# Pulling the down-projection turns of a segment apart by up units, and counting GpSimd's transfers in the kernel's own scheduler

## The chip, the cores and the metric

The kernel runs on one core of a Trainium2 chip. The metric is the device time of one execution in microseconds (us), lower is better; each value below is the median of runs of the same program. The core has five engines with their own instruction queues: TensorE (PE, with its weight loads shown as PEld), VectorE (DVE), ScalarE (ACT), GpSimd (POOL) and SyncE (SP). In this kernel SP issues the loads of weights, and POOL issues the transfers that add into DRAM.

## The reference: what is computed

One decoder block on 256 tokens of width 2048, all in float32. A conditioning vector c gives six vectors of shift, scale and gate (`mod = silu(c) @ w_ada + b_ada`).

```
h = modulate(rms_norm(x), sh1, sc1);  proj = h @ w_in          # 2048 -> 6144: q k v, and gb gc xt
attn = causal attention of 8 heads with normalised q, k;  conv = gb * causal_dwconv(gc * xt)
x = x + g1 * (concat(rms_norm(attn), rms_norm(conv)) @ w_out)
h2 = modulate(rms_norm(x), sh2, sc2)
u = causal_dwconv(h2 @ w_ffn_up);  u_gate, u_up = split(u)     # 2048 -> 11264
x = x + g2 * ((silu(u_gate) * u_up) @ w_ffn_down)              # 5632 -> 2048
```

## The kernel before

Every product is made from two halves of each operand: a weight tile `raw` of 1 MB is loaded by SP, ACT rounds it to `hi` (L299, `split_hi`), DVE subtracts to get `lo` (L308, `split_lo`), and PE adds three products (hi times hi, hi times the rest of the other operand, lo times hi). The activations are split in the same way.

The work is a list of 208 *steps* (the code calls them `slots`), each with one weight tile and its matmuls, in the order in which PE runs them:

- 48 steps of `w_in`, in the order of `CFG['turns']`. An entry names a 512-column group (`q0`, `q1`, `k0`, ...; a bare letter means both groups at once) and a range of 128-row blocks of the input. A group whose next entry is more than three steps away (`near`) has its sum taken out of PSUM: `evac_in` copies it the first time (ACT) and adds to it afterwards (DVE, L502).
- 16 steps of `w_out`. Here the attention, the short convolution and the second normalisation run beside the matmuls.
- 12 steps that begin six *up units* (units 0 to 5, the first half of the input rows).
- From step 76 on (`F0`), the order of `CFG['plan']`. An integer is an up unit: 512 columns of `w_ffn_up`, four steps of 4 blocks (two for units 0 to 5, which have begun), into four PSUM banks `z`. Units 2n and 2n+1 hold the gate and the up part of the same columns, so the pair gives two *groups* (2n and 2n+1) of rows for the down projection. A pair `(seg, fp)` is a *down turn*: it multiplies the groups of one segment with one half (fp) of the columns of `w_ffn_down`. Segments 0, 1, 2 have 8, 6 and 4 groups; the last 4 groups go through the *tail*, eight steps at the end.

In a down turn a group is done either with a step `c` (24 matmuls), or, for the letter `S` in `CFG['forms']`, with a seven-product scheme in two steps: `r` (9 matmuls), then sums of the weight blocks on DVE in place (`sums_of`, L319 to L321), then `T` (12 matmuls). A turn fills eight banks; each is copied by ACT (`evac_q`, L907) and added by POOL into a DRAM accumulator (L909). After the last segment POOL reads the eight sums of a half back (`load_q`, L923), DVE joins them to four tiles (`join`, L931), `gate_down` multiplies them by the gate g2 (L963, L965), and POOL adds the output rows.

When an up unit's last step is through, a *chain* turns its banks into operands of the down projection: `up_sum_a` copies on ACT (L804), `up_sum_v` adds on DVE (L816), `up_conv` on ACT (L842, L840) and `up_taps` on DVE (L856), `up_gate` on DVE (L864), `up_hi` on ACT (L868), `up_lo` on DVE (L872, it writes `gl`). `up_sum_v` is what frees the four banks.

The conditioning weights `w_ada` are interleaved: an entry of `CFG['ada']` is [which of the six, first block, columns, on PE, first step, span, ...]; its tiles are loaded by SP and consumed by DVE (L375, L377) or PE. For the last gate g2 (entry 5) the two numbers are the first and the last up unit beside which it is consumed. The gate g2 is then spread over the partitions by two matmuls in front of four chosen up steps, `CFG['spread']`, pairs of [unit, its step]: a bank is taken, PE writes it (L1715, L1716), and ACT copies it out (L1724, `spread_copy`), which frees the bank.

From step 76 on, the order of the instructions on ACT, DVE and POOL is chosen at build time by a list scheduler in the kernel. Every operation is an `Op` with an engine, a cost, what it depends on, a due time, and the banks and tiles it takes and frees. At each turn of its loop it takes, on each engine, the operation that could start now with the earliest due time:

```python
            start = max([clock[o.e], o.nb] + [d.end + (0.05 if d.e != o.e else -1.0 if d.e == "PE" else 0.0) for d in o.deps] + [sorted(res[k])[n - 1] for k, n in o.need.items() if n]
                        + ([landed.get(o.key, 0.0)] if o.key is not None else []))
            late = max(0.0, start - clock[o.e] - CFG["slack"])
            rank = (late > 0, late if late > 0 else o.due)
```

When a weight tile will have landed is guessed by `arrive`: each load takes 2.7 us of one DMA clock. The engines then run what they were given in that order, whatever really lands when. There are 8 PSUM banks, 6 buffers for `raw`, and in the scheduler's account 12 small tiles.

Of the kernel before, what the change touches and what calls it, by code (L numbers as in the profile page):

```python
# [16 lines left out]
S = 256  # L17
# [11 lines left out]

CFG = {'ada': [[0, 12, 512, False, 17, 4], [4, 8, 512, False, 66, 9], [0, 4, 512, True, 4, 6],
# [4 lines left out]
 'bufs': [38, 6, 6, 3, 5],  # L37
# [5 lines left out]
 'fill': [[3, 12]],  # L43
 'fill_at': [0, 14, 11],
 'tr3': 0,
 'keep': {},
 'spin': [0, 0, 0, 0, 0, 0],
 'plan': [6, 0, 1, 7, 2, 3, 8, 4, 5, 9, (0, 0), (0, 1), 10, 11, 12, 13, 14, 15, (1, 0), (1, 1), 16, 17, 18, 19, (2, 1), (2, 0), 20, 21],
 'tail': [(0,36,4),(1,36,4),(2,36,4),(0,40,4),(1,40,4),(2,40,4),(3,36,4),(3,40,4)],
 'slack': 0.05,  # L50
 'taps': [1, 0, 0],
 'utaps': 2,
 'utlag': 1,
 'sslag': 1,
 'split': [6, 8],
 'segs': [8, 6, 4, 4],
 'forms': ['cScScScc', 'cScScc', 'cScc'],
 'back_q': [-17, -12],
 'join': [30.0, 10.0],
 'tiles': 12,  # L60
 'free0': 4,
 'spread': [[19, 2], [19, 3], [20, 2], [20, 3]],
 'heads': [2, 7, 8, 4, 5, 5, 4, 4],
 'head_steps': [1, 1, 2, 3, 5],
 'conv': [[1, 3, 3, 2, 6, 9, 8, 9], [1, 2, 3, 2, 1, 3, 5, 5]],
# [11 lines left out]
 'tr': [3, 7, 2],  # L77
 'part': 2,
 'up': [[0, 2, 3], [0, 2, 3], [0, 2, 3], [0, 2, 3]],
 'gate': [30, 30, 10, 10],  # L80
 'cls': {'add': 2,
         'h2_rest': 1,
         'att_n': 1,
# [45 lines left out]
 'direct': [4, 0],  # L129
 'spill': [8, 2],  # L130
 'back': [-10, -9, -1, -6],
 'x_first': [1, 2, 3, 4, 5, 9, 10, 12, 13, 15, 16, 19, 21, 23, 24, 28, 31, 39, 43, 45, 46, 48, 49, 50, 51, 55, 56,
             58, 59, 64, 65],
 'h_act': True,
 'h_lag': 0,
 'hi_late': [5, 8, 12, 14, 15, 16, 17, 18, 19, 20, 21, 23, 27, 28, 35, 39, 40, 45, 49, 53, 56, 58, 61, 65, 66, 67, 68, 72, 74, 76, 77, 78, 80, 81, 82, 84, 85, 86, 88, 89, 90, 92, 93, 94, 120, 122, 123, 125, 126, 127, 129, 133, 134, 136, 137, 138, 139, 143, 163, 165, 166, 167, 169, 171, 172, 174, 190, 191, 193, 195, 198, 199, 201, 202, 204],
 'first_hi': True,
 'xn_ahead': [6],
 'cut': [4, 4],
# [5 lines left out]
def tile_block(  # L145
# [138 lines left out]

    splits, halfway = [], []

    kind, held, ready_w = {}, {}, {}

    def half_tile(tag, i):
        t, n = (tag, N_HL) if i < DEEP or (i - DEEP) % 4 else ("raw", N_RAW)  # L290
        return sb.tile([P, 4, 512], F32R, tag=t, bufs=n, name=tag)

    def split_hi(nk, gate=None, i=0):
        t = held.pop(i - 1) if kind.get(i) == "T" else take(slots[i][0] if clock else None)
        if gate is not None and not clock:
# [148 lines left out]
    slots, tasks, extra = [], {}, {}  # L444
# [163 lines left out]
    def rows_of(t, f):  # L608
        return out[0, t * P:(t + 1) * P, f * 512:(f + 1) * 512]
# [294 lines left out]
    def evac_q(seg, fp, n):  # L904
        if True:
            e = t2k(f"e{fp}{n}")
            act(e, qb.pop((seg, fp, n)), AF.Copy, scale=-1.0 if n in ("a", "c00", "c10") else 1.0)  # L907
            if (fp, n) in qd:
                nc.gpsimd.dma_start(qd[fp, n], e, accum_op=ALU.add)  # L909
            else:  # L910
                qd[fp, n] = dram.tile([P, 512], F32, name=f"q{fp}{n}")
                nc.gpsimd.dma_start(qd[fp, n], e)

# [44 lines left out]
    def gate_down(f):  # L958
        assert (G2, f) in gB
        for t in range(2):  # L960
            d = dacc[t, f]
            if f % 2:
                V.tensor_tensor(out=d, in0=d, in1=gB[G2, f], op=ALU.mult)  # L963
            else:
                V.scalar_tensor_tensor(out=d, in0=d, scalar=-1.0, in1=gB[G2, f], op0=ALU.mult, op1=ALU.mult)  # L965
            if f < 2:
                nc.gpsimd.dma_start(rows_of(t, f), d, accum_op=ALU.add)
            else:
                nc.gpsimd.dma_start(d, rows_of(t, f), accum_op=ALU.add)
# [10 lines left out]
    def down_turn(seg, fp, ga, form):  # L980

        a11, a12, a22 = (1, 0), (0, 0), (0, 1)
        todo = []
        for i, e in enumerate(form):
            g = ga + i

            def tok(j, t, g=g):
                return tuple(v[:, t * P:(t + 1) * P] for v in gT[2 * g + j])

            if e == "c":  # L990
                todo.append(("c", [(f"c{t}{f}", (tok, j, t), 2 * j + f) for f in range(2) for t in range(2) for j in range(2)], g))
            else:
                todo.append(("r", [("a", (tok, *a11), 2), ("c00", (tok, *a12), 0), ("c01", (sT, g, 3), 1)], g))
                todo.append(("T", [("c10", (tok, *a22), 0), ("7", (sT, g, 1), 1), ("6", (sT, g, 2), 2), ("5", (sT, g, 0), 3)], g))
        first, last = {}, {}
        for i, (_, ps_, _) in enumerate(todo):
            for j, (n, _, _) in enumerate(ps_):
# [64 lines left out]
        a += n  # L1062
    F0 = N_OUT + NS * cut[0] // 4
    for (a, b), form in zip(SEGS, CFG["forms"]):
        assert b - a == len(form)
        seven |= {a + i for i, e in enumerate(form) if e == "S"}
        for n, g in enumerate(sorted(seven & set(range(a, b)))):
            wide_st[g] = n < 3
    for grp in range(NS):
# [567 lines left out]

    done_1 = {}
    up_ops(F0 - 1)
    for i in range(F0, len(slots)):  # L1640
        j = i + LA
        for j in ([j] if j < len(slots) else []):
            raw = slots[j][0]
            nk = slots[j][1]
            d = [pe.get(j - 4)]
            if kind.get(j) == "T":
                d.append(sum_op[j - 1])
            if j in gated:
# [27 lines left out]
        for seg, fp, n in outs_at.get(i, []):  # L1676
            if fp is None:
                f = n
                Op("DVE", 1.3 if f < 3 else 1.5, lambda f=f: evac_down(f), [pe[i], prev["gB", f]] + (g_op["gd", f] if f > 1 else []), due=tid[i + 1] + 5,
                   free={"b": 2}, need={"t": 2}, out=2 if f < 2 else 0)  # L1680
            else:
                a = Op("ACT", 0.48, lambda seg=seg, fp=fp, n=n: evac_q(seg, fp, n), [pe[i]], need={"t": 1}, free={"b": 1}, out=1)
                freeing.append((i, a, 1))
                prev["q", fp] = a
            if (seg, n) == (len(CFG["forms"]) - 1, "c11"):
                b = None
                for r in range(3):
# [124 lines left out]
```

## Time and profile before

| | |
|---|---|
| time before, median of 3 runs | 1169.33 us (1168.83 to 1169.68) |
| the profiled execution, own time | 1167.0 us |
| its span, first to last instruction | 1165.2 us |
| mean granted TensorE clock | 0.998 of full speed |
| PE busy | 1143.1 us (98%) |
| DVE / ACT / POOL busy | 960.6 / 733.9 / 68.2 us |
| DMA | 334.76 MB, mean 287 GB/s |

The profiled execution is 2.3 us shorter than the median of the runs without a profile, and its time is 1.8 us longer than its span.

### The profile page before, as it was taken

Reading aid. Unit: us, or ns where it says so; the run is one execution under the profiler, and the core shown is the slowest. Engines: PE = TensorE matmul, PEld = TensorE weight load, DVE = VectorE, ACT = ScalarE, POOL = GpSimd, SP = SyncE. Lnnn points to the kernel's source line nnn. Section 1 sums busy time; section 2 is a strip of 40 time slices with the busy share of each in tenths; the row PEclk is TensorE's granted clock in tenths of the full one; section 3 lists DMA queues with packets and bytes.
Section 4 is the critical chain, followed back from the end, with each engine's and each line's share of the span. In section 5 each row is a group of like instructions: output and inputs, shape, how many; then the busy total and the mean of one; then the engine's idle time right before and its main releaser. Section 6 shows DMA issues by size and latency. Waiting matters only on the chain.

```text
span 1165.2 us, 15759 instructions
## 1 busy us (share of the span) xinstructions
PE 1143.1 (98%) x6079; PEld 967.0 (83%) x6079; DVE 960.6 (82%) x996; ACT 733.9 (63%) x1134; POOL 68.2 (6%) x100
## 2 busy tenths in 40 slices
PE   5999999999999999999999999999999999999998
PEld 3677778888887889988888888888888888888787
DVE  4889989999999978878888987589878658775685
ACT  6645365567785565569879765477666648674551
POOL 1000000000000000000000001100001210014302
PEclk9999999999999999999999999999999999999999
DMA  9999989999899799965564576888767997569965
GB/s 363 406 415 412 408 321 367 385 346 346 288 341 339 254 329 324 384 222 181 183 201 161 179 262 236 327 327 288 266 213 218 262 302 278 198 178 315 306 249 108
DMA packets 140442, 334.76 MB, mean 287 GB/s; under 512 B 6592, under 2 KB 15252, under 8 KB 136016
## 3 DMA queue, kind: packets, MB, share of 16 engines
q1 hardware_dynamic: 129728, 311.45, 74.0%
q0 software_dynamic: 9344, 20.17, 7.6%
q10 hardware_dynamic: 1296, 2.16, 0.5%
q8 instruction: 47, 0.77, 0.2%
q14 instruction: 27, 0.22, 0.1%
HBM read 315.92 MB, written 17.83 MB: 286 GB/s over the span
## 4 chain that ended last, share of the span: by engine, by line
PE 88%; DMA 7%; DVE 2%; ACT 2%; issue 1%; SPq 0%; DVEq 0%; ACTq 0%
PE z L1044 24%; PE z L1047 12%; PE z L1030 4%; PE qc L1008 3%; PE qc L1007 3%; PE qc L1006 3%; DMA raw<-in_w_ffn_up_dram 2%; DMA raw<-in_w_ada_dram 2%; DVE lo L308 1%; DMA raw<-in_w_ffn_down_dram 1%; PE mk L490 1%; PE mk L491 1%; PE mk L488 1%; PE ada L371 1%; PE mq L490 1%; PE mq L491 1%
## 5 line engine op out<-in xcount | busy, mean ns | idle before, releaser
L308 DVE TENSOR_TENSOR lo<-raw,hi 128x2048 fp32r<-128x2048 f32 (+1 forms) x207 | 465.9, 2257 | 107.5 <-ACT hi L299 104.3
L299 ACT ACTIVATE hi<-raw 128x2048 fp32r<-128x2048 f32 (+1 forms) x207 | 390.3, 1892 | 251.6 <-DMA raw<-in_w_ffn_up_dram 60.2
L1044 PE MATMUL z<-h,hi 128*128 128x512 f32 x1280 | 301.0, 392 | 2.1 <-ACT ada L1724 2.1
L1044 PEld LDWEIGHTS z<-h,hi 128*128 128x128 f32 x1280 | 238.7, 189 | 50.6 <-ACT ada L1724 2.5
L377 DVE SCALAR_TENSOR_TENSOR ada<-raw,csil,ada 128x512 f32<-128x512 f32 (+3 forms) x167 | 195.6, 1176 | 23.4 <-DMA raw<-in_w_ada_dram 19.9
L1047 PEld LDWEIGHTS z<-h,lo 128*128 128x128 f32 x1280 | 159.2, 192 | 3.3
L1047 PE MATMUL z<-h,lo 128*128 128x256 f32 x1280 | 160.4, 283 | 0.0
L1008 PE MATMUL qc<-lo,gh 128*128 128x512 f32 x216 | 84.2, 390 | 0.2 <-DVE lo L308 0.2
L1006 PE MATMUL qc<-hi,gl 128*128 128x512 f32 x216 | 84.0, 389 | 0.0
L1007 PE MATMUL qc<-hi,gh 128*128 128x512 f32 x216 | 84.0, 389 | 0.0
L840 ACT ACTIVATE tap<-ub,fc 128x256 f32<-128x256 f32 x176 | 75.0, 505 | 0.0
L856 DVE TENSOR_TENSOR uy<-tap,uy 128x510 f32<-128x510 f32 x88 | 60.2, 687 | 8.3 <-ACT tap L840 3.8
L804 ACT ACTIVATE ub<-z 128x256 f32<-128x256 f32 x112 | 34.4, 385 | 39.4 <-PE z L1044 33.1
L842 ACT ACTIVATE uy<-ub,fc,fc 128x256 f32<-128x256 f32 x88 | 48.1, 601 | 9.9 <-DVE ub L816 7.7
L1008 PEld LDWEIGHTS qc<-lo,gh 128*128 128x128 f32 x216 | 40.6, 188 | 9.4 <-DVE lo L308 1.1
L1007 PEld LDWEIGHTS qc<-hi,gh 128*128 128x128 f32 x216 | 40.6, 188 | 8.4
L1006 PEld LDWEIGHTS qc<-hi,gl 128*128 128x128 f32 x216 | 40.5, 188 | 8.4
L1030 PE MATMUL z<-h,hi 128*128 128x256 f32 x256 | 46.6, 284 | 0.4 <-ACT h L740 0.2
L1030 PEld LDWEIGHTS z<-h,hi 128*128 128x128 f32 x256 | 40.0, 192 | 0.8 <-ACT h L740 0.5
L816 DVE TENSOR_TENSOR ub<-z,ub 128x256 f32<-128x256 f32 x96 | 33.9, 416 | 7.6 <-ACT ub L804 7.6
L1030 PE MATMUL z<-h,lo 128*128 128x256 f32 x128 | 36.2, 283 | 0.0
L355 POOL MEMSET ada<- 128x2048 f32 x2 | 3.6, 1814 | 517.4 <-DVE lo L308 438.2
(509 smaller groups left out, 1776.4 us busy)
## 6 DMA issues: line engine op xcount, KB each, us to landing
raw<-in_w_ada_dram SPq DMA_DIRECT2D x96, 1024.0 KB, 7.0
raw<-in_w_ffn_up_dram SPq DMA_DIRECT2D x88, 1024.0 KB, 5.2
raw<-in_w_in_dram SPq DMA_DIRECT2D x47, 1024.0 KB, 7.9
raw<-in_w_ffn_down_dram SPq DMA_DIRECT2D x44, 1024.0 KB, 6.3
raw<-in_w_out_dram SPq DMA_DIRECT2D x16, 1024.0 KB, 6.3
q<-e POOLq DMA_DIRECT2D x18, 256.0 KB, 7.2
q0c<-e0c POOLq DMA_DIRECT2D x12, 256.0 KB, 8.0
q1c<-e1c POOLq DMA_DIRECT2D x12, 256.0 KB, 7.5
```

The costliest lines, as they stand in the source:

```text
L299: act(hi[:, :nk], t[:, :nk], AF.Copy)
L308: V.tensor_tensor(out=lo[:, :nk], in0=t[:, :nk], in1=hi[:, :nk].bitcast(F32), op=ALU.subtract)
L377: V.scalar_tensor_tensor(out=self.acc, in0=t[:, j, :], scalar=csil[:, i:i + 1], in1=self.acc, op0=ALU.mult, op1=ALU.add)
L840: act(z[d - 1][:, s], ub[unit][w][:, s], AF.Copy, scale=fcols[2 - d][:, i:i + 1])
L842: act(y[:, s], ub[unit][w][:, s], AF.Identity, bias=fcols[3][:, i:i + 1], scale=fcols[2][:, i:i + 1])
L856: V.tensor_tensor(out=pair(y)[:, :, d:], in0=pair(z[d - 1])[:, :, :256 - d], in1=pair(y)[:, :, d:], op=ALU.add)
L1006: mm(qb[seg, fp, n], y, hi[:, b], start=first[n] == (i, j), stop=False)
L1007: mm(qb[seg, fp, n], x, hi[:, b], start=False, stop=False)
L1008: mm(qb[seg, fp, n], x, lo[:, b], start=False, stop=last[n] == (i, j))
L1030: mm(o, w[:, j, a], h2T[k + j][:, v * 256:v * 256 + 256], start=begins and j == 0 and w is hi and not v, stop=ends and j == 3 and w is lo)
L1044: mm(zp[grp][ft], hi[:, j, ft * P:(ft + 1) * P], h2T[k + j], start=begins and j == 0, stop=ends and j == 3)
L1047: mm(zp[grp][ft][:, :256], lo[:, j, ft * P:(ft + 1) * P], h2T[k + j][:, :256], start=False, stop=False)
```

## The change

The list of steps is permuted, and the scheduler is told of more. No operation of the arithmetic is added; the counts of matmuls are the same. Part by part:

- `plan`: unit 10 moves between the two turns of segment 0, units 18 and 19 move between the two turns of segment 2, the turns of segment 1 change places, and units 0 and 6 change places at the start.
- `forms`: in segment 1 the seven-product steps are groups 2 and 4 of the turn in place of 1 and 3.
- `spread`: the steps [19, 2], [19, 3], [20, 2], [20, 3] become [19, 2], [20, 1], [20, 2], [21, 2].
- `moved`: the scheduler's DMA clock is advanced by 1.4 us for each of POOL's adding transfers and by 0.65 us for each of its plain ones.
- `load_q` depends on all eight copies of the turn, not on the last one made; `join` of the second half may come 13 us after its turn in place of 10; `gate_down` of block 1 is due later (42 for 30); the scheduler's `slack` is 0.1 for 0.05.
- `turns`: the first two entries change places; `g1` and `k1` move up and `v` 2 to 4 moves down among the early ones; `x0` 8 to 16 moves up by four steps. `ada`: four entries start or end one or two steps (units) earlier or later. `x_first` and `hi_late` (the order of ACT's rounding within a step) change in a few numbers.
- New letters `r` and `T` in a form would allow the two steps of a group to be apart; the forms in use don't have them.

```diff
-CFG = {'ada': [[0, 12, 512, False, 17, 4], [4, 8, 512, False, 66, 9], [0, 4, 512, True, 4, 6],
-         [5, 0, 2048, False, 9, 17], [3, 8, 512, False, 54, 8], [1, 4, 512, False, 3, 7],
+CFG = {'ada': [[0, 12, 512, False, 18, 3], [4, 8, 512, False, 64, 9], [0, 4, 512, True, 4, 6], [4, 0, 1024, False, 23, 22],
+         [0, 8, 512, True, 11, 12], [0, 2, 256, True, 0, 5], [5, 0, 2048, False, 8, 16], [3, 8, 512, False, 54, 7],
...
- 'turns': [['g', 0, 2], ['c', 0, 2], ['v', 0, 2], ['x', 0, 2], ['q', 0, 4], ['c', 2, 4], ['k', 0, 4], ['g', 2, 4],
-           ['x', 2, 4], ['x1', 4, 8], ['x0', 4, 8], ['v', 2, 4], ['g1', 4, 8], ['k1', 4, 8], ['v0', 4, 8],
+ 'turns': [['c', 0, 2], ['g', 0, 2], ['v', 0, 2], ['x', 0, 2], ['q', 0, 4], ['c', 2, 4], ['k', 0, 4], ['g', 2, 4],
+           ['x', 2, 4], ['x1', 4, 8], ['g1', 4, 8], ['x0', 4, 8], ['k1', 4, 8], ['v', 2, 4], ['v0', 4, 8],
...
- 'plan': [6, 0, 1, 7, 2, 3, 8, 4, 5, 9, (0, 0), (0, 1), 10, 11, 12, 13, 14, 15, (1, 0), (1, 1), 16, 17, 18, 19, (2, 1), (2, 0), 20, 21],
+ 'plan': [0, 6, 1, 7, 2, 3, 8, 4, 5, 9, (0, 0), 10, (0, 1), 11, 12, 13, 14, 15, (1, 1), (1, 0), 16, 17, (2, 1), 18,
+          19, (2, 0), 20, 21],
- 'slack': 0.05,
+ 'slack': 0.1,
...
- 'forms': ['cScScScc', 'cScScc', 'cScc'],
+ 'forms': ['cScScScc', 'ccScSc', 'cScc'],
- 'join': [30.0, 10.0],
+ 'join': [30.0, 13.0],
- 'spread': [[19, 2], [19, 3], [20, 2], [20, 3]],
+ 'spread': [[19, 2], [20, 1], [20, 2], [21, 2]],
...
- 'gate': [30, 30, 10, 10],
+ 'gate': [30, 42, 10, 10],
...
+    def moved(us):
+
+        clock["DMA"] = max(clock["DMA"], clock["now"] + 1.0) + us
...
             if (fp, n) in qd:
                 nc.gpsimd.dma_start(qd[fp, n], e, accum_op=ALU.add)
+                moved(1.4)
             else:
+                moved(0.65)
...
             nc.gpsimd.dma_start(t, qd[fp, n])
+            moved(0.65)
...
                 nc.gpsimd.dma_start(d, rows_of(t, f), accum_op=ALU.add)
             else:
                 nc.gpsimd.dma_start(d, rows_of(t, f), accum_op=ALU.add)
+                moved(1.4)
...
-                prev["q", fp] = a
-            if (seg, n) == (len(CFG["forms"]) - 1, "c11"):
+                left_q.setdefault((seg, fp), []).append(a)
+            if seg == len(CFG["forms"]) - 1 and len(left_q[seg, fp]) == 8:
...
-                    a = Op("POOL", (3.0, 2.0, 3.0)[r], lambda fp=fp, r=r: load_q(fp, r), [prev["q", fp], b],
+                    a = Op("POOL", (3.0, 2.0, 3.0)[r], lambda fp=fp, r=r: load_q(fp, r), left_q[seg, fp] + [b],
```

## Rows read from the trace of the kernel before

**Rows 1.** Part 1 of the page: busy time of an engine, its share of the span, instructions.

```profile
PE 1143.1 (98%) x6079; PEld 967.0 (83%) x6079; DVE 960.6 (82%) x996; ACT 733.9 (63%) x1134; POOL 68.2 (6%) x100
```

**Rows 2.** The list of waits of PE over the whole span: who waited for whom, total us, times, longest.

```profile
PE ada L371 <- DMA raw<-in_w_ada_dram: 9.2, 3, 7.3
PE pv_ccol L212 <- DMA vcb<-in_c_dram: 4.0, 1, 4.0
PE z L1044 <- ACT ada L1724: 2.1, 1, 2.1
...
PE qc L1008 <- DVE lo L308: 0.2, 1, 0.2
```

**Rows 3.** The timeline of PE in units 20 and 21 (start, duration, what, count, and in brackets the idle time before it and what ended it). A line merges neighbours of one kind.

```profile
1077.67 0.40 PE L1715 MATMUL adab<-adah,onesr 128*128 128x512 f32 x1
...
1083.74 0.39 PE L1715 MATMUL adab<-adah,onesr 128*128 128x512 f32 x1
...
1086.11 4.50 PE L1044 MATMUL z<-h,hi 128*128 128x512 f32 x19
1092.71 4.82 PE L1044 MATMUL z<-h,hi 128*128 128x512 f32 x13 [2.10 <-ACT ada L1724]
1097.36 2.92 PE L1047 MATMUL z<-h,lo 128*128 128x256 f32 x23
```

**Rows 4.** The same view in unit 14 and 15, where PE doesn't wait.

```profile
841.38 4.00 PE L1047 MATMUL z<-h,lo 128*128 128x256 f32 x32
845.21 7.44 PE L1044 MATMUL z<-h,hi 128*128 128x512 f32 x32
852.49 4.00 PE L1047 MATMUL z<-h,lo 128*128 128x256 f32 x32
```

**Rows 5.** Busy time by stretches of 1 us around the wait: the stretch, its length, busy us (instructions) of PE, PEld, DVE, ACT, POOL, then the granted TensorE clock, the busy share of the DMA engines and GB/s.

```profile
1091.00:1092.00 1.00, 0.00 (x0) 0.00 (x0) 1.00 (x2) 1.00 (x1) 0.00 (x0) 1.00 1.06 414
...
1093.00:1094.00 1.00, 1.00 (x3) 0.81 (x3) 1.00 (x1) 1.00 (x1) 1.00 (x3) 0.50 0.66 256
1094.00:1095.00 1.00, 1.00 (x4) 0.71 (x4) 1.00 (x2) 1.00 (x3) 1.00 (x4) 0.50 0.88 154
...
1096.00:1097.00 1.00, 1.00 (x6) 0.81 (x5) 1.00 (x2) 0.00 (x0) 1.00 (x3) 0.91 0.98 133
```

**Rows 6.** The timeline of ACT over the same stretch.

```profile
1084.77 1.92 ACT L299 ACTIVATE hi<-raw 128x2048 fp32r<-128x2048 f32 x1 [4.09 <-DMA raw<-in_w_ffn_up_dram]
1086.59 0.58 ACT L1724 ACTIVATE ada<-adab 128x512 f32<-128x512 f32 x1
1090.26 1.91 ACT L299 ACTIVATE hi<-raw 128x2048 fp32r<-128x2048 f32 x1 [3.08 <-DMA raw<-in_w_ffn_up_dram]
1092.08 0.58 ACT L1724 ACTIVATE ada<-adab 128x512 f32<-128x512 f32 x1
```

**Rows 7.** The DMA view of 1040 to 1095 us: queue, packets, MB, share of the time of 16 engines (q1 is SP's, q0 is POOL's), and an issuing group with its count, KB each and median us from issue to landing.

```profile
q1 hardware_dynamic: 5103, 10.74, 53.1%
q0 software_dynamic: 2997, 6.40, 52.6%
...
raw<-in_w_ffn_up_dram SPq DMA_DIRECT2D x8, 1024.0 KB, 12.0
```

**Rows 8.** The same view of 960 to 1040 us, where POOL's queue moved nothing.

```profile
q1 hardware_dynamic: 6549, 17.22, 61.3%
...
raw<-in_w_ffn_up_dram SPq DMA_DIRECT2D x8, 1024.0 KB, 5.2
```

**Rows 9.** The chains behind unit 17 (968 to 996 us) and unit 21 (from 1115 us), from the timelines of PE, ACT and DVE. In the first row 16 matmuls are the end of unit 17 and 16 the start of unit 18; the chain does two groups, so a row with x2 or x4 holds one or both.

```profile
975.31 7.44 PE L1044 MATMUL z<-h,hi 128*128 128x512 f32 x32
...
982.28 1.16 ACT L804 ACTIVATE ub<-z 128x256 f32<-128x256 f32 x4
...
988.15 1.47 DVE L856 TENSOR_TENSOR uy<-tap,uy 128x510 f32<-128x510 f32 x2
989.66 0.69 DVE L864 TENSOR_TENSOR uy<-uy,uy 128x512 f32<-128x512 f32 x1
...
994.59 1.29 DVE L872 TENSOR_TENSOR gl<-uy,gh 128x512 fp32r<-128x512 f32 x2
...
1115.86 1.19 ACT L804 ACTIVATE ub<-z 128x256 f32<-128x256 f32 x4
...
1118.19 1.41 DVE L816 TENSOR_TENSOR ub<-z,ub 128x256 f32<-128x256 f32 x4
...
1118.72 1.10 ACT L842 ACTIVATE uy<-ub,fc,fc 128x256 f32<-128x256 f32 x2
1119.70 1.71 ACT L840 ACTIVATE tap<-ub,fc 128x256 f32<-128x256 f32 x4
...
1128.64 1.13 ACT L868 ACTIVATE gh<-uy 128x512 fp32r<-128x512 f32 x2
...
1130.57 1.29 DVE L872 TENSOR_TENSOR gl<-uy,gh 128x512 fp32r<-128x512 f32 x2
```

**Rows 10.** Of the early part: the only wait of PE from 55 to 440 us; the adds of `evac_in` into one letter's sums (min/median/max ns, first and last start); DVE's `lo` for step 66 with the idle time before it; three of the four DVE instructions that consume one 512-column tile of `w_ada`.

```profile
PE z L1030 <- ACT h L740: 0.2, 1, 0.2
...
L502 DVE TENSOR_TENSOR pa_g<-mg,pa_g x12: 680/682/685, 91.7 to 327.4; 128x512 f32<-128x512 f32 x12
...
437.52 4.58 DVE L308 TENSOR_TENSOR lo<-raw,hi 128x2048 fp32r<-128x2048 f32 x2 [2.29 <-ACT hi L299]
...
446.16 2.33 DVE L377 SCALAR_TENSOR_TENSOR ada<-raw,csil,ada 128x512 f32<-128x512 f32 x3
```

More of the change, by code (lines that the diff above doesn't have):

```diff
@@ L47 @@
  'spin': [0, 0, 0, 0, 0, 0],
- 'plan': [6, 0, 1, 7, 2, 3, 8, 4, 5, 9, (0, 0), (0, 1), 10, 11, 12, 13, 14, 15, (1, 0), (1, 1), 16, 17, 18, 19, (2, 1), (2, 0), 20, 21],
- 'tail': [(0,36,4),(1,36,4),(2,36,4),(0,40,4),(1,40,4),(2,40,4),(3,36,4),(3,40,4)],
- 'slack': 0.05,
+ 'plan': [0, 6, 1, 7, 2, 3, 8, 4, 5, 9, (0, 0), 10, (0, 1), 11, 12, 13, 14, 15, (1, 1), (1, 0), 16, 17, (2, 1), 18,
+          19, (2, 0), 20, 21],
+ 'tail': [(0, 36, 4), (1, 36, 4), (2, 36, 4), (0, 40, 4), (1, 40, 4), (2, 40, 4), (3, 36, 4), (3, 40, 4)],
+ 'slack': 0.1,
  'taps': [1, 0, 0],
@@ L131 @@
  'back': [-10, -9, -1, -6],
- 'x_first': [1, 2, 3, 4, 5, 9, 10, 12, 13, 15, 16, 19, 21, 23, 24, 28, 31, 39, 43, 45, 46, 48, 49, 50, 51, 55, 56,
-             58, 59, 64, 65],
+ 'x_first': [1, 2, 3, 4, 5, 9, 10, 12, 13, 15, 16, 20, 21, 23, 24, 28, 31, 39, 43, 45, 46, 48, 49, 50, 51, 55, 56, 58,
+             59, 64, 65],
  'h_act': True,
  'h_lag': 0,
- 'hi_late': [5, 8, 12, 14, 15, 16, 17, 18, 19, 20, 21, 23, 27, 28, 35, 39, 40, 45, 49, 53, 56, 58, 61, 65, 66, 67, 68, 72, 74, 76, 77, 78, 80, 81, 82, 84, 85, 86, 88, 89, 90, 92, 93, 94, 120, 122, 123, 125, 126, 127, 129, 133, 134, 136, 137, 138, 139, 143, 163, 165, 166, 167, 169, 171, 172, 174, 190, 191, 193, 195, 198, 199, 201, 202, 204],
+ 'hi_late': [5, 8, 12, 15, 16, 17, 19, 20, 21, 23, 27, 28, 35, 39, 40, 45, 49, 53, 55, 56, 58, 61, 65, 66, 67, 68, 72,
+             74, 76, 77, 78, 80, 81, 82, 84, 85, 86, 88, 89, 90, 92, 93, 94, 120, 122, 123, 125, 126, 127, 129, 133,
+             134, 136, 137, 138, 139, 143, 163, 165, 166, 167, 169, 171, 172, 174, 190, 191, 193, 195, 198, 199, 201,
+             202, 204],
  'first_hi': True,
@@ L285, in tile_block @@
     splits, halfway = [], []
-    kind, held, ready_w = {}, {}, {}
+    kind, held, ready_w, opener = {}, {}, {}, {}
     def half_tile(tag, i):
@@ L293, in split_hi @@
     def split_hi(nk, gate=None, i=0):
-        t = held.pop(i - 1) if kind.get(i) == "T" else take(slots[i][0] if clock else None)
+        t = held.pop(opener[i]) if kind.get(i) == "T" else take(slots[i][0] if clock else None)
         if gate is not None and not clock:
@@ L982, in down_turn @@
         a11, a12, a22 = (1, 0), (0, 0), (0, 1)
-        todo = []
-        for i, e in enumerate(form):
-            g = ga + i
+        todo, g, begun = [], ga, []
+        for e in form:
             def tok(j, t, g=g):
@@ L991, in down_turn @@
                 todo.append(("c", [(f"c{t}{f}", (tok, j, t), 2 * j + f) for f in range(2) for t in range(2) for j in range(2)], g))
-            else:
+            if e in "rS":
                 todo.append(("r", [("a", (tok, *a11), 2), ("c00", (tok, *a12), 0), ("c01", (sT, g, 3), 1)], g))
-                todo.append(("T", [("c10", (tok, *a22), 0), ("7", (sT, g, 1), 1), ("6", (sT, g, 2), 2), ("5", (sT, g, 0), 3)], g))
+                begun.append((("T", [("c10", (tok, *a22), 0), ("7", (sT, g, 1), 1), ("6", (sT, g, 2), 2),
+                                     ("5", (sT, g, 0), 3)], g), len(slots) + len(todo) - 1))
+            if e in "TS":
+                t, o = begun.pop(0)
+                opener[len(slots) + len(todo)] = o
+                todo.append(t)
+            if e != "T":
+                g += 1
+        assert not begun
         first, last = {}, {}
@@ L1064, in tile_block @@
     for (a, b), form in zip(SEGS, CFG["forms"]):
-        assert b - a == len(form)
-        seven |= {a + i for i, e in enumerate(form) if e == "S"}
+        assert b - a == len(form.replace("T", ""))
+        seven |= {a + i for i, e in enumerate(form.replace("T", "")) if e in "rS"}
         for n, g in enumerate(sorted(seven & set(range(a, b)))):
@@ L1639, in tile_block @@
     up_ops(F0 - 1)
+    left_q = {}
     for i in range(F0, len(slots)):
@@ L1646, in tile_block @@
             if kind.get(j) == "T":
-                d.append(sum_op[j - 1])
+                d.append(sum_op[opener[j]])
             if j in gated:
@@ L1680, in tile_block @@
                    free={"b": 2}, need={"t": 2}, out=2 if f < 2 else 0)
+                continue
             else:
```

7 rows, old and new, of the table CFG are left out of this document.

## The prediction

> **What bounds the kernel now.** I read the busy shares first, then the waits of PE, then the pitch of its matmuls, and last the timelines around the one long wait. PE is busy for 98% of the span [rows 1], but a busy row can hide stalls, since a matmul's record is longer than its pitch. So the pitch decides: where PE doesn't wait, 32 matmuls of 512 columns take 852.49 - 845.21 = 7.28 us from the first start to the next kind's first start, 0.2275 us each, and 32 of 256 columns take 3.83 us, 0.12 us each [rows 4]. A full step of an up unit (16 of each) is thus 5.56 us, and no order of the same matmuls makes it less. What an order can win is only the time in which PE doesn't keep this pitch.
>
> The waits say where that is [rows 2]. Of about 16 us, 13.2 lie at the start (the first vector and the first `w_ada` tiles), before anything this change moves can matter. From 55 to 440 us PE waits 0.2 us in all [rows 10]. After that there is one wait of any size: 2.1 us for ACT's `spread_copy` (L1724). Another of 0.2 us is for a `lo` in a down turn.
>
> The timeline of PE gives the whole price of that wait [rows 3]. The 32 matmuls of 512 columns that end unit 20 and begin unit 21 start at 1086.11, the next kind at 1097.36: 11.25 us for what takes 7.28 elsewhere [rows 4], so 3.97 us are lost. 2.10 of them are the wait. The rest is slow matmuls behind it: 13 in 4.65 us where 13 x 0.2275 = 2.96 would do. The granted clock was 1.00 in the idle stretch and 0.50, the 1.2 GHz level, for the stretches after 1093, back towards 1.00 in 1096 to 1097 [rows 5]: PE had been idle for 2.1 us before it fell, and at work again since 1092.71 when it rose.
>
> Why the wait: PE needs the fourth bank of unit 21, and the bank is still held by a spread sum. The two last spreads were made at 1077.67 and 1083.74 [rows 3], but ACT copied them out at 1086.59 and 1092.08, over 8 us later each [rows 6]. Ahead of each copy in ACT's order stands a rounding of `raw` that waits for its load, 4.09 and 3.08 us. The loads are late because from 1040 to 1095 POOL's queue takes 52.6% of the DMA engines' time beside SP's 53.1%, and a 1 MB load takes 12.0 us from issue to landing [rows 7]; without POOL's traffic it took 5.2 [rows 8]. That traffic is the sums of two adjacent turns of segment 2 and their reading back.
>
> **The change, part by part.**
>
> *`spread`.* The copies at [20, 2] and before now have two steps, 2 x 5.56 = 11.1 us, until unit 21 asks for its fourth bank. Even if a copy again starts 8.9 us after its spread began (1086.59 - 1077.67) and takes 0.58, it ends 1.6 us ahead. The one at [21, 2] is wanted back only in the tail, more than 11 us later, since unit 20's four banks are free by then. Worth: 3.97 us, the whole loss; if the copy were late by two steps, 0. I take 3.97. The four pairs of matmuls are the same as before, 0.
>
> *Units 18 and 19 between the turns of segment 2, and `join` at 13.* POOL's 6.40 MB of 1040 to 1095 are some 24 transfers of 256 KB, 52.6% of 55 us = 28.9 us of all engines, 1.2 us each. Eight adds and eight reads back of the first turn leave this stretch: 19 of 28.9 us. The loads of units 20 and 21 should then land in 5 to 8 us. That gives PE nothing beyond the 3.97 us, since it has no other wait there. The moved 19 us fall in units 18 and 19, four steps each, 44 us.
>
> *Segment 2 directly behind unit 17.* This is the price I fear. The turn `cScc` uses unit 17's first group in its third weight block, that is after 24 + 9 + 12 = 45 matmuls, 10.2 us after unit 17's end. Its chain, by its own durations, is 1.19 + 1.41 + 2.69 (L842 and L840, 1118.72 to 1121.41) + 1.47 + 0.69 + 0.6 + 0.68 = 8.7 us [rows 9]: no stall. As it ran before, the first `gl` was done 16.3 us after unit 17's end (978.95 to 995.27), and for unit 21 15.4 us after the chain began [rows 9]: a stall of 5.2 to 6.1 us. Neither had to hurry: group 16 was wanted 8 x 5.56 + 10.2 = 54.7 us later, and unit 21's groups after three steps of the tail, 72 x 0.2275 = 16.4 us, and were ready just then. So the scheduler fits a chain to its due time, and I take a value near the lower end: 10.7 us, a stall of 0.5. Both ends stay for the range.
>
> *Unit 10 between the turns of segment 0, segment 1's order and forms.* PE lost 0.2 us in all the down turns by the list of waits [rows 2]. At most that is won; the cover is what ACT and DVE have ready, and if it fails in one step the cost is that step's lateness. 0.
>
> *`moved`, `left_q`, `slack`, `gate`.* They change the order that the scheduler writes, not an operation. Where PE keeps its pitch this is worth 0, and at most the 3.97 us counted above; a wrong order costs what the next part but one says.
>
> *Early turns and loads.* One `evac_in` fewer adds twice 0.682 us less on DVE [rows 10]; PE waits 0.2 us in this stretch, so it is worth 0 to 0.2. The first tile of `w_ada` entry [4, 8] is now consumed ahead of step 66's `lo`: some 3.1 us (2.33 for three of four instructions) where DVE idled 2.29 [rows 10], so that `lo` ends about 0.8 us later; for PE the bounds are 0 and 3.1 us, and I take 0, since DVE's idle time takes three quarters of it and PE shows no wait on DVE here. Unit 0 wants the upper half of the normalised input two steps sooner than unit 6 did, and the entry that feeds it is moved two steps up: 0. g2's tiles end one unit sooner, which helps unit 17.
>
> Sum against the profiled execution: 1167.0 - 3.97 + 0.5 = 1163.5. The runs without a profile lie 2.3 us above it, which I carry over: 1169.33 - 3.5 = 1165.8.
>
> **The rivals.**
>
> *The chain is late* (slower). If unit 17's chain runs as slowly as both chains on record, PE stalls 5.2 to 6.1 us and, as behind the wait of 2.1 us, 1.7 us more at the lower clock: 1169.33 - 3.97 + 6.9 to 7.8 = 1172.3 to 1173.2. For it: the record. Against it: the due times. It decides from a chain of 14.8 us on (stall 4.6 + 1.7 = 6.3); between 11.5 and 14.8 the result is no change.
>
> *The jam moves.* POOL's 19 us of transfers meet the loads of units 18 and 19, those land late, and the copy for [19, 2] or the release of a unit's banks waits behind them on ACT as before. It costs what it cost there, about 4 us: 1169.3 to 1169.8. For it: the two queues took even shares of the engines whatever their sizes [rows 7]. Against it: from 960 to 1040 SP's queue used 61.3% [rows 8], so there is room for most of the 19 us in 44. The Trainium skill, "DMA: Bandwidth & Descriptors", section "Queues, rings and completion order", states that each engine takes turns between the queues that have work, a packet at a time. The even shares above agree. By that rule alone the collision isn't removed but moved, and the sum would be this rival's.
>
> *It doesn't do what it says.* Another copy stands behind a late load and the same wait stays at unit 21: 1169.3. The 1.6 us to spare speak against it.
>
> *More is won.* The new order also clears the 0.2 us waits and something at the start: 1163.5 to 1164.5.
>
> **How the numbers follow.** Forecast case (wait gone, new stalls under 1.5 us) 0.52, its own range 1164.5 to 1167.0; chain late 0.15, a third of it between the signs; jam moves 0.15; wait stays 0.08; more won 0.07; early part 1 to 2 us worse, 0.03. A measurement tells this kernel from no change at about 0.2%, 2.3 us: below 1167.0 is faster, above 1171.7 slower. Faster: 0.52 + 0.07 and a little of the jam, 0.60. Slower: two thirds of the late chain and a little, 0.13. Same: 0.27. The range leaves out the late chain and the lower half of "more won": 1164.0 to 1171.0.
>
> **What would show it.** PE's list of waits without `ada L1724`, the clock 1.00 around unit 21, loads of units 20 and 21 at 5 to 8 us, and POOL's bytes spread over both stretches. A wait of PE in the turn behind unit 17 on `gl` (L872) shows the late chain, one in units 18 and 19 on ACT the moved jam. The forecast is wrong if either is above 2 us, or if PE waits between 60 and 500 us for more than 1 us.

## The result, and the profile after

After takes 1162.38 us (1161.86 to 1162.58, 6 runs), and before beside it 1168.93 (1167.28 to 1169.68, 6 runs); over the 93 runs of before that the experiments below added, it takes 1167.4 (1165.1 to 1170.6). The ratio is 0.9945 [0.9932, 0.9958], and in a second comparison (e13, after unchanged, expected at 1161.9 to 1162.6) 0.9954 [0.9941, 0.9968]: some 5 us, 0.5% faster, and faster than the range that I gave. The profiled execution of after has a span of 1160.8 us and an own time of 1162.58, against 1165.2 and 1167.0.

The busy times on the page, and under them the list of waits of PE over the whole span, as in [rows 1, 2]:

```profile
PE 1141.7 (98%) x6079; PEld 967.2 (83%) x6079; DVE 959.3 (83%) x994; ACT 734.0 (63%) x1134; POOL 67.8 (6%) x100
```

```profile
PE ada L378 <- DMA raw<-in_w_ada_dram: 8.6, 3, 7.5
PE pv_ccol L215 <- DMA vcb<-in_c_dram: 4.3, 1, 4.3
PE mq L497 <- DVE adaz L415: 0.6, 1, 0.6
PE mc L559 <- ACT h L1516: 0.4, 1, 0.4
PE z L1048 <- ACT h L747: 0.3, 1, 0.3
```

The line for L1724 is gone, and so is the 0.2 us for `lo` in a down turn. In this profile nothing behind 430 us waits any more (the second profile of after, e13's, has one wait of 0.3 us for a `lo` at 737 us). The timelines of PE and ACT through units 20 and 21 (L1062 is before's L1044, L1744 its L1724) answer [rows 3, 6]:

```profile
1077.66 0.40 PE L1735 MATMUL adab<-adah,onesr 128*128 128x512 f32 x1
...
1085.64 7.44 PE L1062 MATMUL z<-h,hi 128*128 128x512 f32 x32
1092.92 4.00 PE L1065 MATMUL z<-h,lo 128*128 128x256 f32 x32
```

```profile
1080.64 1.92 ACT L306 ACTIVATE hi<-raw 128x2048 fp32r<-128x2048 f32 x1 [5.17 <-DMA raw<-in_w_ffn_up_dram]
1082.46 0.58 ACT L1744 ACTIVATE ada<-adab 128x512 f32<-128x512 f32 x1
```

The 32 matmuls at the unit's border take 1092.92 - 1085.64 = 7.28 us, the undisturbed pitch of [rows 4], where before took 11.25. The copy still stands behind a rounding that waits 5.17 us for its load, and comes 4.8 us after its sum, but nobody wants that bank yet. The DMA view of 1040 to 1095 us, and then of 990 to 1040, answers [rows 7, 8]:

```profile
q1 hardware_dynamic: 4884, 9.71, 50.6%
q0 software_dynamic: 1744, 3.66, 31.6%
...
raw<-in_w_ffn_up_dram SPq DMA_DIRECT2D x8, 1024.0 KB, 7.7
```

```profile
q0 software_dynamic: 1792, 4.20, 33.3%
...
raw<-in_w_ffn_up_dram SPq DMA_DIRECT2D x6, 1024.0 KB, 12.0
```

POOL's bytes are spread over both stretches, and the slow loads have moved: 7.7 us for units 20 and 21 (12.0 before), 12.0 for units 18 and 19. Last, the chain behind unit 17, which answers [rows 9]: PE's timeline, where the first row begins the turn and the second is the first matmul that needs unit 17's first group, and then DVE's.

```profile
978.94 0.39 PE L1024 MATMUL qc<-hi,gl 128*128 128x512 f32 x1
...
989.14 0.39 PE L1024 MATMUL qc<-hi,gl 128*128 128x512 f32 x1
```

```profile
987.25 0.68 DVE L879 TENSOR_TENSOR gl<-uy,gh 128x512 fp32r<-128x512 f32 x1
```

The first `gl` is done at 987.93, 9.0 us after the unit's end at 978.94. PE wants it at 989.14, so 1.2 us are to spare.

### The profile page after: what moved, and what is told of

The parts are those of the page before. It is cut to its first block, busy times and chain, and to the rows that moved or that the text cites. A ratio compares the mean times of both kernels' runs of the same rounds, so it can differ in the third digit from the quotient of the medians.

```text
span 1160.8 us, 15739 instructions
## 1 busy us (share of the span) xinstructions
PE 1141.7 (98%) x6079; PEld 967.2 (83%) x6079; DVE 959.3 (83%) x994; ACT 734.0 (63%) x1134; POOL 67.8 (6%) x100
## 4 chain that ended last, share of the span: by engine, by line
PE 94%; DMA 3%; DVE 1%; ACT 1%; issue 0%; SPq 0%; DVEq 0%; ACTq 0%
PE z L1062 25%; PE z L1065 13%; PE qc L1025 4%; PE qc L1024 4%; PE qc L1026 4%; PE z L1048 4%; DMA raw<-in_w_ada_dram 2%; PE mk L497 1%; PE mk L498 1%; PE mk L495 1%; PE ada L378 1%; PE mq L497 1%; PE mq L498 1%; PE mq L495 1%; PE mv L497 1%; PE mc L497 1%
## 5 line engine op out<-in xcount | busy, mean ns | idle before, releaser
L1062 PE MATMUL z<-h,hi 128*128 128x512 f32 x1280 | 299.5, 390 | 0.0
L1062 PEld LDWEIGHTS z<-h,hi 128*128 128x128 f32 x1280 | 237.7, 188 | 47.8
```

What stands on the lines that cost most here:

```text
L1062: mm(zp[grp][ft], hi[:, j, ft * P:(ft + 1) * P], h2T[k + j], start=begins and j == 0, stop=ends and j == 3)
```

## The experiments

All times are medians. Kernels e1 to e4, e5 to e8, e9 to e12, e13 to e16 and e17 to e18 ran together, each group on one chip, with before beside them at 1167.04, 1167.45, 1167.79, 1167.49 and 1167.39.

**Where the 2.3 us lie: e1**, before unchanged.

> The kernel before, unchanged, for the span and the clock of each of its runs and for a second profile. Theory A: the 2.3 us by which the runs of before exceed its profiled execution are longer stalls at late loads, in the program itself. Then time minus span is 1.8 us in every run, as in both profiles so far, the spans spread from 1165 to 1168, and the longer ones have a mean clock below 0.998. Theory B: they lie around the program (launch, measuring). Then the spans stay within 0.5 us of 1165.2 and time minus span is 2 to 4 us in the longer runs.

Measured: 1167.02 (1165.11 to 1169.53, 12 runs). Over the 93 runs of before the spans go from 1163.3 to 1168.7 and time minus span has a median of 1.86 us (86 of the 93 lie between 1.79 and 2.2, the longest is 3.1). The 21 runs with a span under 1164.5 have a mean clock of 0.9997, the 33 of 1166 or more 0.9972. The second profile shows where most of it goes: the list of waits of PE, PE's timeline, then ACT's.

```profile
PE z L1044 <- ACT ada L1724: 3.8, 1, 3.8
```

```profile
1087.02 4.50 PE L1044 MATMUL z<-h,hi 128*128 128x512 f32 x19
...
1099.97 4.00 PE L1047 MATMUL z<-h,lo 128*128 128x256 f32 x32
```

```profile
1088.57 1.92 ACT L299 ACTIVATE hi<-raw 128x2048 fp32r<-128x2048 f32 x1 [5.28 <-DMA raw<-in_w_ffn_up_dram]
1090.39 0.58 ACT L1724 ACTIVATE ada<-adab 128x512 f32<-128x512 f32 x1
1092.85 1.91 ACT L299 ACTIVATE hi<-raw 128x2048 fp32r<-128x2048 f32 x1 [1.88 <-DVE lo L308]
1094.66 0.58 ACT L1724 ACTIVATE ada<-adab 128x512 f32<-128x512 f32 x1
```

The same wait, 3.8 us for 2.1, in a span 2.5 us longer: theory A. The 32 matmuls at the border take 1099.97 - 1087.02 = 12.95 us where the first profile had 11.25, so 1.7 of the 2.5 us lie there, and most of the rest at the first loads. The first of the two roundings waits for its load, the second for DVE's `lo` of the tile before, and so for the same late load. Before is not a kernel of 1169.3 with a fixed cost around its program: its span itself differs from run to run, and in both profiles the longest wait behind the start hangs on a late load. The runs without a profile show only their span and clock, so that the loads make all of their spread isn't shown.

**Which part removes the wait: e2 to e4.**

e2, before with the new spread alone:

```diff
- 'spread': [[19, 2], [19, 3], [20, 2], [20, 3]],
+ 'spread': [[19, 2], [20, 1], [20, 2], [21, 2]],
```

> Before with nothing changed but the four places of the spread. Theory A (the spread's bank, waited for at unit 21, is the whole loss of before, and the loss is longer in most runs than in its profile): 1162.0 to 1163.5, 6 us under before, no wait of PE for ACT's copy, runs within 0.7 us of each other. Theory B (the offset of 2.3 us lies around the program): 1169.0 - 4.0 = 1165.0, give or take 0.5. Rival C (the spread alone isn't enough, since POOL's traffic keeps the loads late and another wait takes its place): 1167 or more, with a wait of PE for ACT or for hi between 1070 and 1130.

Measured: 1163.52 (1163.26 to 1163.90), ratio 0.9966 [0.9954, 0.9978]; no wait for the copy, though the up loads take 11.5 us. The wait is cured, as theory A said; a rest of about 1 us to after stays.

e3, before with the turns of segment 2 pulled apart alone, and e4, after with the old spread:

```diff
- ... 16, 17, 18, 19, (2, 1), (2, 0), 20, 21]
+ ... 16, 17, (2, 1), 18, 19, (2, 0), 20, 21]
```

> Before with units 18 and 19 between the two turns of segment 2 and nothing else changed: the old places of the spread. Theory (the relief of the loads isn't needed where the spread is moved, but is enough by itself): POOL's queue falls from 52.6% to 30 to 35% of the stretch of units 20 and 21, the copies start under 5 us after their sums, the bank is back before unit 21 asks for it: 1162.5 to 1164.5. Rival: with the old places the copy is still late, since fewer steps lie between: a wait of 0.5 to 2 us at unit 21 stays, 1165 to 1168. The second rival of the prediction (chain behind unit 17 late): a wait of PE for gl of over 2 us in the turn behind unit 17.

> After, with the old places of the spread. If the pulled-apart turns suffice by themselves: as after, 1162.0 to 1163.0, with no wait for the copy. If the spread carries the gain: the wait at unit 21 is back, with 1 to 2 us of PE idle and 1 to 1.7 us at the lower clock: 1164.5 to 1166.

Measured: e3 1169.99, ratio 1.0021 [1.0011, 1.0030]; e4 1162.61. In e3 the copy is in time, but the rival of the late chain is there, as the list of waits of PE and then DVE's timeline show:

```profile
PE qa L1006 <- DVE ub L816: 3.3, 1, 3.3
PE qc L1006 <- DVE gl L872: 2.2, 1, 2.2
```

```profile
942.84 2.35 DVE L377 SCALAR_TENSOR_TENSOR ada<-raw,csil,ada 128x2048 f32<-128x2048 f32 x1 [5.82 <-DMA raw<-in_w_ada_dram]
...
954.82 2.35 DVE L377 SCALAR_TENSOR_TENSOR ada<-raw,csil,ada 128x2048 f32<-128x2048 f32 x1 [4.78 <-DMA raw<-in_w_ada_dram]
...
965.88 2.35 DVE L377 SCALAR_TENSOR_TENSOR ada<-raw,csil,ada 128x2048 f32<-128x2048 f32 x1 [4.19 <-DMA raw<-in_w_ada_dram]
...
982.84 0.69 DVE L321 TENSOR_TENSOR raw<-raw 128x512 f32<-128x512 f32 x1
...
987.78 1.41 DVE L816 TENSOR_TENSOR ub<-z,ub 128x256 f32<-128x256 f32 x4
```

ACT in e3, and the sums of weights on DVE in after (its L328 is e3's L321):

```profile
983.62 1.92 ACT L299 ACTIVATE hi<-raw 128x2048 fp32r<-128x2048 f32 x1 [3.65 <-DVE raw L321]
985.45 1.18 ACT L804 ACTIVATE ub<-z 128x256 f32<-128x256 f32 x4
```

```profile
973.70 0.69 DVE L328 TENSOR_TENSOR raw<-raw 128x512 f32<-128x512 f32 x1
```

DVE stands idle three times for a tile of g2, and all that is queued behind, the turn's sums of weights (L321) too, comes 9 us later than in after (982.84 for 973.70). ACT waits for those sums with a rounding, and unit 17's `up_sum_a` (L804) stands behind that. So e4's gain needs something else of after besides the turns.

**What lets the turns be pulled apart: e5, e6, e9.** One number pair, put into e3 (e5), taken back out of after (e6), and put into before by itself (e9); the rest of the line is left out:

```diff
-         [5, 0, 2048, False, 9, 17], ...
+         [5, 0, 2048, False, 8, 16], ...
```

> As e3 (before, with units 18 and 19 between the turns of segment 2), and the conditioning entry of g2 one unit earlier (8 to 16 for 9 to 17), nothing else. Theory G: in e3 DVE came 9 us late to the end of unit 17, because its instructions that consume the tiles of g2 waited 5.82, 4.78 and 4.19 us for their loads until 966 us; one unit earlier they are through by 945 and the chain behind unit 17 is in time: no wait of PE for ub or gl there, 1162.5 to 1163.8. Rival S (the chain is fitted to a due time that the scheduler of before gets wrong, and the new account of transfers or the slack mends it): the stalls of 3.3 and 2.2 us stay, 1168.5 to 1170.5.

> After, with the conditioning entry of g2 back at units 9 to 17. Theory G: the chain behind unit 17 is late as in e3, 4 to 7 us of stall there with the clock at half rate behind it: 1166.5 to 1170. Rival S: as after, 1162 to 1163.

> Before, with the conditioning entry of g2 one unit earlier and nothing else: the turns of segment 2 stay adjacent, the spread stays. Theory: by itself it is worth nothing, since in before nobody waits for the chain of unit 17; POOL's jam and the wait for the copy at unit 21 stay: 1166.5 to 1168.5, with runs spread over 2 us or more. Rival: g2's tiles are the late loads' partners, and the copy comes in time once they are gone: 1163 to 1164.

Measured: e5 1162.88, 0.9961 [0.9947, 0.9974]; e6 1172.66, 1.0040 [1.0024, 1.0056]; e9 1167.35, 1.0001 [0.9992, 1.0010]. The waits of PE in e6, and in e9:

```profile
PE qc L1024 <- DVE gl L879: 4.2, 1, 4.2
PE qc L1026 <- DVE lo L315: 2.8, 2, 1.8
PE qa L1024 <- DVE ub L823: 1.3, 1, 1.3
```

```profile
PE z L1044 <- ACT ada L1724: 2.7, 1, 2.7
```

Theory G holds in both directions: the earlier tiles are worth 7 us where the turns are apart (e3 to e5), 10 in after (e6, more than I had expected: a second place, at 724 to 746 us, stalls for `ub` and `lo` too), and nothing where they are adjacent. In e6 DVE's idle times ahead of unit 17's chain are 6.28 and 6.49 us for a `hi` of ACT, not for g2's loads; that g2's entry makes the chain late is shown by the edit there, the way in which it does so only by e3.

**What is left of after: e10, e14, e13, e11, e12, e7.** e10 is e5 with segment 1's new form and order of turns; e14 is the same kernel beside after (e13). From after, e11 takes the early part away, e12 the move of unit 10, e7 the effect of `moved`.

```diff
- 'plan': [... (1, 0), (1, 1), ...],
+ 'plan': [... (1, 1), (1, 0), ...],
- 'forms': ['cScScScc', 'cScScc', 'cScc'],
+ 'forms': ['cScScScc', 'ccScSc', 'cScc'],
```

> As e5 (turns of segment 2 apart, g2 one unit earlier), and segment 1 with after's form and order of turns. The profile of e5 still shows the loss of 0.37 us at 890 us that before has and after hasn't. Theory: that is all that is left between e5 and after: 1162.88 - 0.4 = 1162.5, give or take 0.3, and no loss at 890. Rival: the early part or the new spread also counts, and it stays at 1162.9.

> The kernel of e10 (before with the turns of segment 2 apart, g2 one unit earlier, segment 1's form and order) beside after. Theory: these three edits are the whole gain and the other parts (new spread, early part, unit 10, account of transfers, slack, due times) are worth nothing: within 0.5 us of e13. Rival: what is left out is worth 0.5 us or more, to either side, and e10's 1161.86 against 1162.38 came from chips or chance.

> After, with the early part of before: its turns, conditioning entries (but for g2's), the orders of ACT's rounding, and unit 6 ahead of unit 0. Theory: the early part is worth nothing, 1162.1 to 1162.7. Rivals: it has brought the step from 1162.9 to 1162.4 (then 1162.8 to 1163.3), or cost 0.7 us, as the first loads of after ended later in its profile (then 1161.6).

> After, with unit 10 behind both turns of segment 0 as before. Theory: the jam of POOL's adds is no cost there, since up units follow with time to spare: 1162.2 to 1162.8, PE without a wait at 700 to 760 us. Rival: the loads of units 10 and 11 come late behind 16 adds in a row: 1163 or more, with a wait for hi or lo between 720 and 790 us.

> After, with moved() doing nothing, so that the scheduler's DMA clock counts SP's loads only. Theory: the account of transfers changes the order on ACT and DVE in a few places but PE waits for none of them: 1162.2 to 1163.0, no new wait over 0.5 us. Rival: it is what keeps the copies out of the way of late loads, and a wait of 1 us or more at units 18 to 21 comes back: 1163.5 to 1166.

Measured: e10 1161.86, e14 1162.10, e13 1162.14, e11 1162.23, e12 1161.93, e7 1162.12. Three came out 0.1 to 0.3 us below the ranges that I had given (e7, e10, e12). The loss at 890 us is in the traces of before, e1, e2, e3, e5, e9 and e18, and in none with the new form and order; which of the two clears it wasn't tried. PE in before:

```profile
889.00 0.39 PE L1007 MATMUL qc<-hi,gh 128*128 128x512 f32 x1
889.59 0.50 PE L1008 MATMUL qc<-lo,gh 128*128 128x512 f32 x1 [0.20 <-DVE lo L308]
```

The two starts are 0.59 us apart where the pitch is 0.2275: 0.36 us are lost, of which the list of waits shows 0.2. Until the pitch is back it is 0.5 us. Three edits, the turns apart, g2 one unit earlier and segment 1, are enough for the whole gain (e14 beside e13); the new spread (e4), the early part, unit 10 and `moved`, taken from after one by one, are worth nothing that shows.

**Why the turns apart are not the only way: e8, e16, e15, e17, e18.** e8 puts the two turns of segment 2 side by side again in after. e16 is e8 with `moved` doing nothing, e15 is e8 with the old spread, e17 is e15 with `moved` doing nothing. e18 is before's configuration in after's code, with `moved` counted and the reading back behind all eight copies.

> After, with the two turns of segment 2 adjacent again behind unit 19 (new places of the spread, g2 early, all else of after). Theory: with the spread moved the pulled-apart turns are worth nothing more, since PE has no other wait at the late loads: POOL's share at units 20 and 21 back at 50 to 55%, loads at 11 to 12.5 us, and 1162.2 to 1163.6 as for the spread alone. Rival: late loads hold something else back, 1164.5 or more with a wait for hi, lo or the copy there.

> As e8 (after with adjacent turns), with moved() doing nothing. In e8 DVE's order puts four multiplications of gate_down (2.57 us) ahead of three lo in the tail, and PE lost 3.9 us from 1090 to 1150 waiting for lo; in e2, with the scheduler of before, the lo stand first and PE lost nothing. Theory: the account of POOL's transfers makes that order, since it thinks the tail's loads later than they are; without it the lo stand first again: 1162.2 to 1163.5, under 1 us lost there. Rival: the late loads of adjacent turns alone cost it: 1165 or more.

> After with both the adjacent turns of segment 2 and the old places of the spread. Theory (the wait at unit 21 needs both: late loads and too little room behind the spread): the wait for the copy is back at unit 21, 2 us or more with the clock at half rate behind it, 1165.5 to 1168 and runs spread over 2 us or more. Rival: after's other parts keep the copy in time, 1162.5 to 1163.5.

> As e15 (after with adjacent turns and the old spread, which came out at 1161.84 with no wait), with moved() doing nothing. From the two orders on ACT: in e15 the last two copies of the spread stand behind 6 and 7 roundings counted from the last gate of the turn and ahead of the sums of unit 20; with moved() off they stand behind 7 and 8, as in before. Theory: the account of transfers is a third cure of the same wait, since it lets the scheduler see that the roundings' loads will be late and put each copy one rounding earlier; without it the wait at unit 21 is back: 1165 to 1168, runs spread over 2 us or more. Rival: something else of after (segment 1, early part, unit 10) makes e15 quick: 1161.7 to 1162.5.

> Before's whole configuration with after's code, so that only the account of transfers (and the reading back behind all eight copies) is added. On ACT the last two copies then stand together behind 8 roundings, ahead of the sums of unit 20. Theory: the second copy is no earlier than in before, so the wait stays: 1166 to 1169. Rival: the account alone cures it: 1162 to 1163.5.

Measured, after with adjacent turns:

| | `moved` counted | `moved` off |
|---|---|---|
| new spread | e8: 1165.69 | e16: 1161.92 |
| old spread | e15: 1161.84 | e17: 1166.81 |

e18: 1164.34, 0.9970 [0.9959, 0.9980], with 0.6 us of PE waiting for the copy. My theory for e8 fell (its rival came), the one for e15 fell (no wait, with both the adjacent turns and the old spread, and up loads of 12.9 us), and those for e16 (0.3 us below its range) and e17 held. The one for e18 fell too, but its time is that of neither theory nor rival. ACT in e15, and then in e17:

```profile
1080.14 1.92 ACT L305 ACTIVATE hi<-raw 128x2048 fp32r<-128x2048 f32 x1 [2.72 <-DMA raw<-in_w_ffn_up_dram]
1081.96 0.57 ACT L1743 ACTIVATE ada<-adab 128x512 f32<-128x512 f32 x1
1086.98 1.92 ACT L305 ACTIVATE hi<-raw 128x2048 fp32r<-128x2048 f32 x1 [4.45 <-DMA raw<-in_w_ffn_up_dram]
1088.81 0.58 ACT L1743 ACTIVATE ada<-adab 128x512 f32<-128x512 f32 x1
```

```profile
1079.17 1.92 ACT L305 ACTIVATE hi<-raw 128x2048 fp32r<-128x2048 f32 x1 [5.04 <-DMA raw<-in_w_ffn_up_dram]
1086.88 1.92 ACT L305 ACTIVATE hi<-raw 128x2048 fp32r<-128x2048 f32 x1 [5.78 <-DMA raw<-in_w_ffn_up_dram]
1088.70 0.58 ACT L1743 ACTIVATE ada<-adab 128x512 f32<-128x512 f32 x1
...
1092.97 0.58 ACT L1743 ACTIVATE ada<-adab 128x512 f32<-128x512 f32 x1
```

The roundings start at the same times in both, 1080 and 1087; with `moved` each copy stands one rounding earlier in the order, and 4 us of lateness are gone. In e18 both copies stand behind one rounding, which itself waits for a `join` on DVE (L938), the first where before has it and the second one rounding earlier than in before (I had counted it at the same place):

```profile
1088.19 1.92 ACT L303 ACTIVATE hi<-raw 128x2048 fp32r<-128x2048 f32 x1 [8.22 <-DVE l L938]
1090.01 1.06 ACT L1741 ACTIVATE ada<-adab 128x512 f32<-128x512 f32 x2
```

That is in time but for 0.6 us. Where the turns are apart and the spread is old, the order isn't what differs: counted from the end of ACT's list, 10 and 9 roundings follow the last two copies in e4, e5, e10 and e14, as in before. There the roundings themselves come sooner, with up loads of 8.1 to 9.7 us in place of 12.0; e14's last copy:

```profile
1087.64 0.57 ACT L1724 ACTIVATE ada<-adab 128x512 f32<-128x512 f32 x1
```

It starts 4.4 us ahead of before's (1092.08). In e8 the account of transfers hurts. DVE in the tail, e8 and then e16 (L974 and L972 are `gate_down`):

```profile
1125.60 1.29 DVE L974 SCALAR_TENSOR_TENSOR l0c<-l0c,ada 128x512 f32<-128x512 f32 x2
...
1128.01 1.28 DVE L972 TENSOR_TENSOR l0c<-l0c,ada 128x512 f32<-128x512 f32 x2
1129.21 6.69 DVE L314 TENSOR_TENSOR lo<-raw,hi 128x2048 fp32r<-128x2048 f32 x3
```

```profile
1123.31 2.29 DVE L314 TENSOR_TENSOR lo<-raw,hi 128x2048 fp32r<-128x2048 f32 x1
...
1126.11 2.28 DVE L314 TENSOR_TENSOR lo<-raw,hi 128x2048 fp32r<-128x2048 f32 x1
...
1130.52 1.29 DVE L974 SCALAR_TENSOR_TENSOR l0c<-l0c,ada 128x512 f32<-128x512 f32 x2
```

In e8 three `lo` are done after the multiplications, and PE waits 1.6 us for one of them; by the starts of its matmuls it loses 1.9 us there, of 3.6 in all behind 1090 us. Most of the rest is for a `lo` at 1094 and at 1113 us, ahead of these rows. None of these versions beats after by more than its runs vary.

## Why the prediction was right or wrong

**The failed step is the last: "which I carry over".** I had three runs of before and a profile, took the 2.3 us between them for a cost of measuring, and added it to a kernel whose stall I had just removed. Time minus span has a median of 1.86 us in before and 1.78 in after: there is no such cost to carry. By e1 the difference lies in the program's own span, which after holds within 0.7 us. The spans of my three runs weren't recorded, so that they had a longer stall is an inference, and they were not typical: of the 93 later runs 7 are as long as their median of 1169.33. Without that step the sum was 1163.5, and every bound of my range would have been 2.3 us lower, 1161.7 to 1168.7.

**The 3.97 us** were right in place and in size: the border of units 20 and 21 runs at pitch. The rest of the way from 1167.0 to after's profiled 1162.58 is 0.45 us net, and it is made of several terms. By the starts of PE's matmuls segment 1 gives 0.85 (below), and what follows the last matmul is 0.46 shorter; against that, after's profile is 0.83 us late from the stretch of the first loads on. In e13's profile that lateness is 0.1, so it belongs to the run and not to the kernel.

**Who removes them** was only half seen. I gave them all to the spread. e2 shows that it is enough, e4 that it isn't needed, and e15 that neither it nor the turns apart are. Two things cure it: copies that stand one rounding earlier in ACT's order (the new spread in e2, `moved` in e15), and roundings that come sooner as their loads do (the turns apart in e4, e5 and e14). One rounding is no guarantee: e18 keeps 0.6 us of the wait.

**The chain behind unit 17** I costed at +0.5; it was 0, with 9.0 us from the unit's end to `gl`, just above my lower bound of 8.7. That the figure came so near was luck. The rival *chain is late* was a true mechanism: e3 and e6 are it, at 1169.99 and 1172.66. I decided it by due times, and what decided it was the entry of g2, of which I wrote that it "helps unit 17" and gave it no price: 7 us (e3 to e5), and 10 in after with the second place that e6 shows.

**Segment 1** I bounded by the 0.2 us in the list of waits. By the starts of PE's matmuls, before's profile loses 0.50 us at 889 and 0.35 at 921, and after's neither: 0.85. The first loss is in every trace with the old form, the second in that one profile only. I had said myself that a busy row hides stalls, and then took the list's number.

**`moved`** I put at 0. In after that is so (e7), but only since two other cures are there; with adjacent turns it changes the time by -5.0 us with the old spread (e17 to e15) and by +3.8 with the new (e16 to e8).

**The early part** is 0, as I said (e11).

***The jam moves*** came half true: the loads of units 18 and 19 went from 5.2 to 12.0 us. The Trainium skill, "DMA: Bandwidth & Descriptors", section "Queues, rings and completion order", has the engines take turns between queues that hold work, and the moved slowness agrees with it. By that rule the time should have stayed, as I had priced the rival; it did not, since PE's list of waits has none in units 18 and 19.

## What to carry to other kernels

A few runs that differ from a profile are not an offset: look at time minus span and at the clock of each run before a difference is carried over, since a stall that hangs on the landing of loads can vary with each run, and its removal then takes the variation along. Engines that run a fixed order turn one late load into a wait for everything behind it, so ask of each in-order wait what stands one place behind it. An edit that moves such a wait away from a tight chain can be worth as much as the chain's whole lateness, as g2's one unit was. Where several edits each cure the same wait, test each alone and each taken away, or the gain is credited to the wrong one.

## What the runs showed of the hardware

One program on one chip varied by 5 us (before beside and in e1: 37 runs, 1165.1 to 1170.6), while after's 11 runs lie within 0.74 us (1161.86 to 1162.60). The longer runs of before have the lower mean granted clock (0.9972 for spans of 1166 us or more, 0.9997 under 1164.5). Its two profiles show a wait of 2.1 and 3.8 us for the copy at unit 21, with a clock of 0.50 behind it.

The clock didn't fall behind every wait, and the longer one doesn't have to be the one behind which it falls. In before it was 0.50 from 1093 to 1096 us, after PE had been idle for 2.10 us, and in e6 from 743 to 745, after 1.77. In e3 it stayed at 1.00 behind an idle time of 3.31 us that ended at 988.25, and was 0.50 from 997 to 1000, after a second one of 2.24 that ended at 995.56. The prediction's 1.7 us at the lower clock is thus no fixed price of a wait.

A 1 MB load took 12.0 us from issue to landing where POOL's queue held 52.6% of the DMA engines' time, and 5.2 where it moved nothing.
